# Ten of eleven feed-forward pairs by Winograd's seven products, where nine were, in a two-layer decoder trunk

## The chip, the cores and the metric

The kernel runs on one core of one Trainium2 chip. The metric is the device time of one execution in microseconds (us). The kernel before was timed three times: 2059.41, 2060.57 and 3379.97 us, median 2060.57 us. The execution that was profiled took 2059.04 us.

## The reference

The input is 512 tokens of 1024 features. Each of two layers computes, in float32,

```
x = LN(ALPHA * x + 0.5 * swiglu(x, ffn1_w13, ffn1_w2))
x = LN(ALPHA * x + mixer(x))
x = LN(ALPHA * x + 0.5 * swiglu(x, ffn2_w13, ffn2_w2))

def swiglu(x, w13, w2):
    a, b = jnp.split(x @ w13, 2, axis=-1)      # each 512 x 2816
    return (jax.nn.silu(a) * b) @ w2
```

So there are four feed-forward blocks (FFN0 and FFN1 in layer 0, FFN2 and FFN3 in layer 1). Between the two of a layer stands the mixer, a gated linear recurrence beside a gated spatial MLP; its last step is a projection of 1024 to 1024 features. The change touches the first half of each feed-forward block, `x @ w13`, and the sums that prepare the second half, `@ w2`.

## The kernel before

**Precision.** Every float32 factor is kept as a rounded part h and a rest l, and a product is three matmuls: h by h, h by l, l by h. `split` makes the parts: ScalarE copies h (L126) and VectorE subtracts it from the source to get l (L127).

**Two kinds of pairs.** The 2816 columns of a and b are 22 blocks of 128, taken as 11 pairs (k and k + 11). A **plain pair** (`proj`, L154) computes for each of its two blocks a (bank `pa`) and b (bank `pb`), each by 24 matmuls of 512 columns. A **pair by seven** (`seven_pairs`, `product`, L553) takes the two blocks, two halves of the features and two halves of the tokens as a 2 by 2 matrix product and computes it by Winograd's seven products; each is 24 matmuls of 256 columns on sums of quarters. For this VectorE adds weight quarters (`PairWeights.sum`, L533), all seven left factors are split (h_pa, l_pa, ...), and the products are combined in `evictions`. The right factors, s1 to s4, are sums of quarters of x; `x_sums` makes them once per block (tiles xr, xs, xs1h, xs1l, ...), after it has added xh and xl to get x back (L479).

**The order of a block.** Before: the pairs 8 and 9 first, as plain pairs; then a section of nine pairs by seven, whose instructions on all engines stand in the order of the program text (`pin`); then `Seven.run` (L354), which multiplies by `w2`, by seven products too. For that, the activations of each pair need sums as well (`activation_sums`, L321 to L332: 5 VectorE subtractions and two splits); three of them ran inside the section, one between the plain pairs, the other seven in `run`. Those of the plain pairs (parts th and tl) go to DRAM through GpSimd's queue and are fetched again. Sums of `w2` quarters are made in DRAM by copying and accumulating DMAs on GpSimd's queue (`sums_in_dram`, L293), one small group every `SUM_GAP` ns of the program's own clock (`Flow`).

**Around it.** Where `pin` doesn't hold, the framework's scheduler orders each engine's instructions by its own estimates. A block's x comes from the norm of the step before, transposed by TensorE per tile of 128 tokens (`to_features`, tr) and split into xh and xl; the new block's first weights (r_a, h_a, l_a and the same for b) are loaded on SP's queue. FFN0 reads x from DRAM already transposed (`first_block`). SP's queue carries all other weights; a tile class "h" of 33 slots holds the large tiles.

Of the kernel before, what the change touches and what calls it, by code (L numbers as in the profile page):

```python
# [28 lines left out]
F32 = mybir.dt.float32  # L29
# [6 lines left out]
P = 128  # L36
D = 1024
# [46 lines left out]
def trunk(ctx: ExitStack, tc, x_in, xt_in, w13, w2, w_in, w_br, w_out, ln_g, ln_b, lb_in, hgn, sgg, sgb, sgws,  # L84
# [30 lines left out]
    xh, xl = [None] * 4, [None] * 4  # L115
# [13 lines left out]
    def weights(src, name, early=False):  # L129

        raw = wk.tile([P, D], F32, tag="raw", name=f"r_{name}", bufs=NRAW)
        nc.sync.dma_start(raw, src)
# [92 lines left out]
    def out_proj(nk, lhs, w_of, c, ln, tag):  # L225

        ys = [[bank(f"y{t}{q}") for q in range(2)] for t in range(NT)]
        w = {}

        def unit(k, t, qs):  # L230
            hi, lo = w[k]
            lh, ll = lhs(k)
            ts = slice(t * P, (t + 1) * P)
            for i, (a, m) in enumerate(((lh, hi), (lh, lo), (ll, hi))):
                for q in qs:
                    PE.matmul(ys[t][q], a[:, ts], m[:, q * 512:(q + 1) * 512],  # L236
                              start=(k == 0 and i == 0), stop=(k == nk - 1 and i == 2))
# [10 lines left out]
        begin_features()  # L248
# [20 lines left out]
    class Seven:  # L269
# [3 lines left out]
        def __init__(self, w_of, order, spilled):  # L273
            self.w_of, self.order, self.spilled = w_of, order, spilled
# [30 lines left out]
        def activation_sums(self, k):  # L305
# [38 lines left out]
        def run(self, c, ln, last, due):  # L344
# [97 lines left out]
            if not last:  # L442
                begin_features()
# [25 lines left out]
    def x_sums(s):  # L469

        lo_t, hi_t = slice(0, 256), slice(256, 512)
        r = {}
        x3 = quads("xs3")
        for c in ("s2", "s1", "s3", "s4"):
            s[c] = tuple(quads(f"x{c}{v}", F32R) for v in "hl")
        for q in range(2):
            for z in (q, q + 2):
                r[z] = slot(f"xr{z}")
                V.tensor_tensor(r[z], xh[z].bitcast(F32), xl[z].bitcast(F32), op=ALU.add)  # L479
            yield 0.0, X_GAP  # L480
# [18 lines left out]
    class PairWeights:  # L499
# [14 lines left out]
        def load(self, to, col, row):  # L514
            for z, j in enumerate((self.k, self.k + NH2)):
                nc.sync.dma_start(to[:, z], self.w13_of(col + j)[:, H[row]])
# [101 lines left out]
    def ffn(l, i, last=False, first_of_all=False):  # L618
        front = [8, 9]
        by_seven = [k for k in range(NH2) if k not in front]  # L620
        order = by_seven[0:2] + front + by_seven[2:]
        seven = Seven(lambda k: w2[l, i, k], order, front)
# [26 lines left out]
        s = {}  # L649
        if first_of_all:  # L650
            glu(js[0], first_block(w13_of(js[0]), w13_of(NF + js[0])))
            s_task = flow.add(x_sums(s), 0.0)
            plain(js[1])
        else:
            first = [blocks(j, True) for j in js[:2]]
            need(0, 1)
            for z, j in enumerate(js[:2]):
# [3 lines left out]
            for z, j in enumerate(js[:2]):  # L661
                pair_of(j, first[z], 256, 256)
                glu(j, first[z])
        seven.activation_sums(front[0])
        for z, j in enumerate(js[2:]):
            args = blocks(j)
            if z == len(js) - 3:
                flow.finish(s_task)
                t = slot("rt")
                cs = [slot(f"rc{v}") for v in range(2)]  # L670
                weights_of = lambda k: PairWeights(w13_of, k, t, cs[by_seven.index(k) % 2])
                pinned[0] = True
                pw = weights_of(by_seven[0])
                pw.load_c()
                pw.load_d()
                pw.sum("t", "a", "b")
                for _ in range(AHEAD):
                    pw.split()
                pw.sum("b", "d", "b")
                pinned[0] = False  # L680
            plain(j, args)
        in_dram = flow.add(seven.sums_in_dram(order))
        pinned[0] = True
        seven_pairs(seven, s, by_seven, weights_of, pw, {0: front[1:2], 2: by_seven[0:1], 3: by_seven[1:2]})
        pinned[0] = False
        flow.finish(in_dram)
        seven.run(0.5 / ALPHA, (l, 2 * i), last, by_seven[2:])

    def gates():

        z = const.tile([P, DEPTH, NH], F32, name="lbz")
        nc.sync.dma_start(z, lb_in)
# [344 lines left out]
    def prepare():  # L1037
        tc.keep_in_program_order(nc.sync.dma_start(tril, tril_in))
        nc.sync.dma_start(ident, ident_in)
# [3 lines left out]
    def first_block(wa, wb):  # L1043

        begin_features()
# [3 lines left out]
        for _ in range(12):  # L1049
# [140 lines left out]
```

## Time and profile before

| what | value |
|---|---|
| median of the three runs | 2060.57 us |
| profiled execution | 2059.04 us, of it span 2057.2 us |
| mean granted TensorE clock | 0.998 of full speed |
| TensorE (PE) busy | 2042.1 us, 99% of the span |
| VectorE (DVE) busy | 1570.1 us, 76% |
| ScalarE (ACT) busy | 930.6 us, 45% |
| GpSimd (POOL) busy | 304.3 us, 15% |
| FFN0: first plain pair, second plain pair, nine pairs by seven | from about 6, 29.50 and 51.26 us; `run` begins at 232.69 us |

A row of the timeline names a tile by the program's name without its number: `xl<-tr,xh` is the split of a transposed bank into xl. Matmuls overlap in PE's pipeline, so the time that one adds to a chain is the distance between two starts, not the duration shown; the same holds, less strongly, on VectorE. A share of 99% says how long PE had work, not that each of its stretches was at its best rate.

### The profile page before, as it was taken

Reading aid. Unit: us, or ns where it says so; the run is one execution under the profiler, and the core shown is the slowest. Engines: PE = TensorE matmul, PEld = TensorE weight load, DVE = VectorE, ACT = ScalarE, POOL = GpSimd, SP = SyncE. Lnnn points to the kernel's source line nnn. Section 1 sums busy time; section 2 is a strip of 40 time slices with the busy share of each in tenths; the row PEclk is TensorE's granted clock in tenths of the full one; section 3 lists DMA queues with packets and bytes.
Section 4 is the critical chain, followed back from the end, with each engine's and each line's share of the span. In section 5 each row is a group of like instructions: output and inputs, shape, how many; then the busy total and the mean of one; then the engine's idle time right before and its main releaser. Section 6 shows DMA issues by size and latency. Waiting matters only on the chain. (4 is left out here: it accounts for less than half of the span.)

```text
span 2057.2 us, 32430 instructions
## 1 busy us (share of the span) xinstructions
PE 2042.1 (99%) x12640; PEld 1840.0 (89%) x12640; DVE 1570.1 (76%) x2357; ACT 930.6 (45%) x1303; POOL 304.3 (15%) x440
## 2 busy tenths in 40 slices
PE   9999999999999999999999999999999999999997
PEld 7999988888888999998899998888888889999986
DVE  7998988943435879889879989879444358898896
ACT  6444565233322544446535446642343225454563
POOL 1222002001000123210112320020010001232001
PEclk9999999999999999999999999999999999999999
DMA  8899586122242479967668986851222425899673
GB/s 264 232 254 233 170 279 231 42 82 82 83 160 96 164 212 237 260 172 252 228 187 236 248 220 192 272 201 52 82 89 86 143 93 191 212 255 239 172 256 136
DMA packets 151049, 375.11 MB, mean 182 GB/s; under 512 B 17136, under 2 KB 17392, under 8 KB 150896
## 3 DMA queue, kind: packets, MB, share of 16 engines
q1 hardware_dynamic: 102672, 242.40, 34.9%
q0 software_dynamic: 48224, 130.64, 26.4%
q8 instruction: 99, 1.62, 0.3%
q14 instruction: 54, 0.44, 0.1%
HBM read 354.10 MB, written 111.15 MB: 226 GB/s over the span
## 5 line engine op out<-in xcount | busy, mean ns | idle before, releaser
L293 POOL DMA_DIRECT2D t<-in_w_dram x176 | 145.5, 905 | 199.5 <-DMA t<-in_w_dram 107.6
L127 DVE TENSOR_TENSOR l_pc<-rc,h_pc 128x1024 fp32r<-128x1024 f32 x72 | 88.0, 1222 | 19.6 <-ACT h_pc L126 19.6
L154 PE MATMUL z<-xh,h_z 128*128 128x512 f32 x256 | 102.6, 401 | 0.0
L154 PE MATMUL z<-xh,l_z 128*128 128x512 f32 x256 | 99.8, 390 | 0.0
L154 PE MATMUL z<-xl,h_z 128*128 128x512 f32 x256 | 99.8, 390 | 0.0
L127 DVE TENSOR_TENSOR l_z<-r_z,h_z 128x1024 fp32r<-128x1024 f32 x32 | 39.2, 1225 | 72.5 <-ACT h_z L126 72.4
L126 ACT ACTIVATE h_pc<-rc 128x1024 fp32r<-128x1024 f32 x72 | 75.7, 1052 | 36.4 <-PE fB L553 34.6
L127 DVE TENSOR_TENSOR l_pa<-ra,h_pa 128x1024 fp32r<-128x1024 f32 x72 | 87.7, 1218 | 1.2 <-ACT h_pa L126 1.2
L553 PE MATMUL fA<-xh,l_pa 128*128 128x256 f32 x288 | 81.5, 283 | 0.0
L553 PE MATMUL fC<-xs1h,h_pt 128*128 128x256 f32 x288 | 81.5, 283 | 0.0
L553 PE MATMUL fC<-xs1l,h_pt 128*128 128x256 f32 x288 | 81.5, 283 | 0.0
L553 PE MATMUL fC<-xs1h,l_pt 128*128 128x256 f32 x288 | 81.5, 283 | 0.0
L553 PE MATMUL fA<-xh,h_pc 128*128 128x256 f32 x288 | 81.5, 283 | 0.0
L553 PE MATMUL fA<-xl,h_pc 128*128 128x256 f32 x288 | 81.5, 283 | 0.0
L553 PE MATMUL fA<-xh,l_pc 128*128 128x256 f32 x288 | 81.5, 283 | 0.0
L553 PE MATMUL fE<-xs3h,h_pb 128*128 128x256 f32 x288 | 81.5, 283 | 0.0
L553 PE MATMUL fE<-xs3l,h_pb 128*128 128x256 f32 x288 | 81.5, 283 | 0.0
L553 PE MATMUL fE<-xs3h,l_pb 128*128 128x256 f32 x288 | 81.5, 283 | 0.0
L553 PE MATMUL fB<-xs2h,h_pa 128*128 128x256 f32 x288 | 81.5, 283 | 0.0
L553 PE MATMUL fB<-xs2l,h_pa 128*128 128x256 f32 x288 | 81.5, 283 | 0.0
L553 PE MATMUL fB<-xs2h,l_pa 128*128 128x256 f32 x288 | 81.5, 283 | 0.0
L553 PE MATMUL fC<-xs4h,h_pd 128*128 128x256 f32 x288 | 81.5, 283 | 0.0
(360 smaller groups left out, 7370.6 us busy)
## 6 DMA issues: line engine op xcount, KB each, us to landing
t<-in_w_dram POOLq DMA_DIRECT2D x88, 512.0 KB, 9.1
t<-t POOLq DMA_DIRECT2D x88, 256.0 KB, 5.5
t<-in_w_dram POOLq DMA_DIRECT2D x88, 256.0 KB, 6.3
r_c<-in_w_dram SPq DMA_DIRECT2D x44, 512.0 KB, 5.1
r_d<-t SPq DMA_DIRECT2D x88, 256.0 KB, 4.1
rd<-in_w_dram SPq DMA_DIRECT2D x72, 256.0 KB, 6.5
ra<-in_w_dram SPq DMA_DIRECT2D x72, 256.0 KB, 5.8
rb<-in_w_dram SPq DMA_DIRECT2D x72, 256.0 KB, 6.5
```

The costliest lines, as they stand in the source:

```text
L126: pin(S.activation(hi, src, AF.Copy))
L127: pin(V.tensor_tensor(lo, src, hi.bitcast(F32), op=ALU.subtract))
L154: PE.matmul(ps[:, n0:n0 + n], a[:, cs], m[:, n0:n0 + n], start=(i == 0), stop=(i == 3 * nk - 1))
L293: tc.keep_in_program_order(nc.gpsimd.dma_start(*of(k), **kw))
L553: PE.matmul(ps[:, half[z]], a[:, ms], v, start=start, stop=(m == 3 and i == 2), skip_group_check=not (first and z == 0))
```

## The change

One pair (10) stays plain and ten are done by seven products. The plain pair's second block and the first pair's weights are put one after the other in the order of the text. `to_features` lets ScalarE copy x itself from the transposed banks into tiles xr (48 copies of 128x2x128 more), and FFN0 loads x straight into xr; the 16 additions of xh and xl go. `x_sums` makes s1 and s3 first, then s2, then s4. Six activation sums run inside the section (behind pairs 0, 1, 3, 4, 6 and 7) and five in `run`. Three pairs' parts (10, 3 and 4) go through DRAM, and those of pair 2 are kept in halves of xl and xh that the section no longer reads. `SUM_GAP` goes from 6000 to 7000, and more of SP's loads are pinned to the order of the text. In all PE issues 288 matmuls more, VectorE 32 tensor operations more, ScalarE 68 activations more, and there are 32 more DMAs.

```diff
-    SUM_GAP = 6000.0
+    SUM_GAP = 7000.0
...
-    def begin_features():
+    def begin_features(whole):
+
         for q in range(4):
             xh[q], xl[q] = slot(f"xh{q}", F32R), slot(f"xl{q}", F32R)
+        for q in range(4):
+            xr[q] = slot(f"xr{q}") if whole else None
...
             for r in range(2):
                 split(xh[2 * q + r][:, :, ts], xl[2 * q + r][:, :, ts], pv[:, r])
+            for r in range(2):
+                if xr[2 * q + r] is not None:
+                    S.activation(xr[2 * q + r][:, :, ts], pv[:, r], AF.Copy)
...
+            elif k in self.home:
+                parts = self.home.pop(k)
...
-                V.tensor_tensor(r[z], xh[z].bitcast(F32), xl[z].bitcast(F32), op=ALU.add)
...
+            V.tensor_tensor(v["s3"][q], r[:, :, lo_t], r[:, :, hi_t], op=ALU.subtract)
+            V.tensor_tensor(v["s1"][q], r[:, :, hi_t], r2[:, :, hi_t], op=ALU.subtract)
+        firsts = [xr[q][:, :, lo_t] for q in range(2)]
...
+        parts("s1")
+        yield 0.0, X_GAP
+        parts("s3")
+        for q in range(2):
+            V.tensor_tensor(v["s2"][q], firsts[q], v["s1"][q], op=ALU.subtract)
+        yield 0.0, X_GAP
+        parts("s2")
+        for q in range(2):
+            V.tensor_tensor(v["s4"][q], v["s4"][q], v["s2"][q], op=ALU.subtract)
+        yield 0.0, X_GAP
+        parts("s4")
...
-        front = [8, 9]
+        front = [10]
...
-        seven = Seven(lambda k: w2[l, i, k], order, front)
+        seven = Seven(lambda k: w2[l, i, k], order, front + by_seven[3:5])
...
         if first_of_all:
-            glu(js[0], first_block(w13_of(js[0]), w13_of(NF + js[0])))
+            pinned[0] = True
+            args = first_block(w13_of(js[0]), w13_of(NF + js[0]))
+            second = blocks(js[1])
+            pinned[0] = False
+            glu(js[0], args)
             s_task = flow.add(x_sums(s), 0.0)
-            plain(js[1])
+            flow.step(s_task)
+            flow.step(s_task)
+            pw = first_weights()
+            plain(js[1], second)
         else:
...
                 pair_of(j, first[z], 256, 256)
                 glu(j, first[z])
...
+                if z == 0:
+                    pw = first_weights()
+        flow.finish(s_task)
+        seven.home[by_seven[2]] = (xl[0][:, 0, 256:512], xl[0][:, 1, 256:512], xh[0][:, :, 256:512], xh[1][:, :, 256:512])
         in_dram = flow.add(seven.sums_in_dram(order))
         pinned[0] = True
-        seven_pairs(seven, s, by_seven, weights_of, pw, {0: front[1:2], 2: by_seven[0:1], 3: by_seven[1:2]})
+        seven_pairs(seven, s, by_seven, weights_of, pw, dict(zip((0, 1, 3, 4, 6, 7), ([v] for v in front + by_seven[0:5]))))
         pinned[0] = False
         flow.finish(in_dram)
-        seven.run(0.5 / ALPHA, (l, 2 * i), last, by_seven[2:])
+        seven.run(0.5 / ALPHA, (l, 2 * i), last, i == 1, by_seven[5:])
```

Three places show how the instructions move. The first is GpSimd's instruction list at the start of the program; its DMAs are issued in this order. `t` are the DRAM tiles of the `w2` sums, `hg` a small parameter of the mixer, th and tl the parts of a plain pair that go to DRAM. Before:

```order
L1186 UNCONDITIONAL_BRANCH
L726 DMA hg<-in_hgn_dram 128x4
L332 DMA th_327<-th_317 128x768
L332 DMA tl_328<-tl_318 128x768
L293 DMA t_75<-in_w_dram 256x512
L293 DMA t_76<-in_w_dram 256x512
L293 DMA t_83<-in_w_dram 256x512
L293 DMA t_75<-in_w_dram 256x1x512
```

With the change:

```order
L1211 UNCONDITIONAL_BRANCH
L299 DMA t_75<-in_w_dram 256x512
L299 DMA t_76<-in_w_dram 256x512
L299 DMA t_85<-in_w_dram 256x512
L299 DMA t_75<-in_w_dram 256x1x512
L299 DMA t_76<-in_w_dram 256x1x512
L299 DMA t_85<-in_w_dram 256x1x512
L752 DMA hg<-in_hgn_dram 128x4
L340 DMA th_481<-th_471 128x768
L340 DMA tl_482<-tl_472 128x768
```

The first group of `w2` copies and adds now stands at the head of the queue, where before it stood behind the parts of the first plain pair.

The second place is VectorE around the first section of FFN0, from the last result of the plain part (`r<-sa,pb`) or the first sum for the pair by seven (`rt`). `l_pa`, `l_pt`, `l_pc` and `l_pb` are the rests of the first pair's first four left factors, the xs tiles the parts of s1 to s4. Before:

```order
L639 TENSOR_TENSOR r_428<-sa,pb_344 128x2x256
L704 TENSOR_TENSOR lb<-lbmx,lbz 128x4
L533 TENSOR_TENSOR rt<-ra_447,rb_448 128x1024
L705 TENSOR_SCALAR om<-lb 128x8
L127 TENSOR_TENSOR l_pa_460<-ra_447,h_pa_459 128x1024
L127 TENSOR_TENSOR l_pt_464<-rt,h_pt_463 128x1024
L127 TENSOR_TENSOR l_pc_468<-rc_445,h_pc_467 128x1024
L533 TENSOR_TENSOR rb_448<-rd_455,rb_448 128x1024
L639 TENSOR_TENSOR r_428<-sa,pb_443 128x2x256
L533 TENSOR_TENSOR ra_447<-ra_447,rb_448 128x1024
L127 TENSOR_TENSOR l_pb_538<-rb_448,h_pb_537 128x1024
```

With the change:

```order
L548 TENSOR_TENSOR rt<-ra_262,rb_263 128x1024
L127 TENSOR_TENSOR l_pa_275<-ra_262,h_pa_274 128x1024
L127 TENSOR_TENSOR xs2l<-xr_113,xs2h 128x512
L127 TENSOR_TENSOR l_pt_279<-rt,h_pt_278 128x1024
L127 TENSOR_TENSOR l_pc_283<-rc_260,h_pc_282 128x1024
L548 TENSOR_TENSOR rb_263<-rd_270,rb_263 128x1024
L127 TENSOR_TENSOR xs2l<-xr_114,xs2h 128x512
L505 TENSOR_TENSOR xr_113<-xr_113 128x2x256
L505 TENSOR_TENSOR xr_114<-xr_114 128x2x256
L654 TENSOR_TENSOR r_238<-sa,pb_235 128x2x256
L127 TENSOR_TENSOR xs4l<-xr_113,xs4h 128x512
L127 TENSOR_TENSOR xs4l<-xr_114,xs4h 128x512
```

The first pair's weight sums and rests now stand between the sums and rests of x, before the last result of the plain part; `ra` and `l_pb` follow behind the rows shown.

The third place is VectorE at the end of layer 0's mixer. `x,sums<-y` adds the mixer's output to x for a tile of tokens, `xl<-tr,xh` splits the transposed x, and l_a, l_b are the rests of the first plain block of FFN1. Before:

```order
L196 SCALAR_TENSOR_TENSOR x_6195,sums<-y_6064,x_6195 128x512
L127 TENSOR_TENSOR l_a_6462<-r_a_6459,h_a_6461 128x1024
L202 TENSOR_SCALAR nm<-sums 128x1
L127 TENSOR_TENSOR l_b_6468<-r_b_6465,h_b_6467 128x1024
L127 TENSOR_TENSOR l_a_6476<-r_a_6473,h_a_6475 128x1024
L208 SCALAR_TENSOR_TENSOR x_6195<-x_6195,nm,lng 128x512 x2
L209 SCALAR_TENSOR_TENSOR x_6195<-x_6195,rstd,lnb 128x512 x2
L127 TENSOR_TENSOR xl_6200<-tr_6379,xh_6199 128x2x128
L127 TENSOR_TENSOR xl_6204<-tr_6391,xh_6203 128x2x128
L196 SCALAR_TENSOR_TENSOR x_6197,sums<-y_6065,x_6197 128x512
```

With the change:

```order
L208 TENSOR_SCALAR nm<-sums 128x1
L214 SCALAR_TENSOR_TENSOR x_6292<-x_6292,nm,lng 128x512 x2
L215 SCALAR_TENSOR_TENSOR x_6292<-x_6292,rstd,lnb 128x512 x2
L127 TENSOR_TENSOR xl_6297<-tr_6484,xh_6296 128x2x128
L127 TENSOR_TENSOR xl_6301<-tr_6498,xh_6300 128x2x128
L202 SCALAR_TENSOR_TENSOR x_6294,sums<-y_6162,x_6294 128x512
L127 TENSOR_TENSOR xl_6299<-tr_6484,xh_6298 128x2x128
L127 TENSOR_TENSOR xl_6303<-tr_6498,xh_6302 128x2x128
L202 SCALAR_TENSOR_TENSOR x_6294,sums<-y_6163,x_6294 128x512
L127 TENSOR_TENSOR l_a_6571<-r_a_6568,h_a_6570 128x1024
L208 TENSOR_SCALAR nm<-sums 128x1
L127 TENSOR_TENSOR l_b_6577<-r_b_6574,h_b_6576 128x1024
```

The rests of the first block's weights now stand behind the last addition of the mixer's output (y_6163); before they stood ahead of the norm of the tile of tokens before it.

## Rows read from the trace of the kernel before

**Rows 1.** The page: span, then busy time of each engine.
```profile
span 2057.2 us, 32430 instructions
PE 2042.1 (99%) x12640; PEld 1840.0 (89%) x12640; DVE 1570.1 (76%) x2357; ACT 930.6 (45%) x1303; POOL 304.3 (15%) x440
```

**Rows 2.** Waits of PE: who for whom, total us, times, longest us.
```profile
PE pE L354 <- DVE l_d L127: 1.6, 4, 0.7
PE pA L354 <- DVE l_c L127: 0.6, 2, 0.3
```

**Rows 3.** Chain of waits in FFN3: start us, us, what; 24 matmuls each.
```profile
1748.81 5.44 PE pa L154 x24
1762.57 2.88 PE fC L553 x24
```

**Rows 4.** PE's timeline: start us, us, line, tile; firsts of stretches.
```profile
29.50 0.39 PE L154 MATMUL pa<-xh,h_a 128*128 128x512 f32 x1
51.26 0.28 PE L553 MATMUL fA<-xh,h_pa 128*128 128x256 f32 x1
232.69 0.40 PE L354 MATMUL pA<-h_b,th 128*128 128x512 f32 x1
715.16 0.40 PE L154 MATMUL pa<-xh,h_a 128*128 128x512 f32 x1
1052.12 0.40 PE L154 MATMUL pa<-xl,h_a 128*128 128x512 f32 x1
```

**Rows 5.** Windows, two pairs: length; PE, PEld, DVE, ACT, POOL busy; clock, DMA.
```profile
100.00:120.00 20.00, 20.00 (x169) 20.00 (x168) 19.28 (x25) 10.11 (x13) 4.14 (x6) 1.00 0.95 228
180.00:200.00 20.00, 20.00 (x169) 20.00 (x168) 17.25 (x19) 9.40 (x11) 4.98 (x6) 1.00 0.91 237
```

**Rows 6.** VectorE's timeline, FFN1: start us, us, line, tiles, shapes.
```profile
712.08 0.68 DVE L127 TENSOR_TENSOR xs4l<-xr,xs4h 128x512 fp32r<-128x512 f32 x1
712.68 0.42 DVE L127 TENSOR_TENSOR tl<-r,th 128x256 fp32r<-128x256 f32 x1
713.02 2.35 DVE L479 TENSOR_TENSOR xr<-xh,xl 128x1024 f32<-128x1024 f32 x2
715.29 0.68 DVE L483 TENSOR_TENSOR xs<-xr 128x512 f32<-128x512 f32 x1
```

**Rows 7.** GpSimd's timeline at the start; in brackets idle time and releaser.
```profile
1.24 0.74 POOL L726 DMA_DIRECT2D hg<-in_hgn_dram  x1 [0.81 <-POOLq L1175]
35.20 0.56 POOL L332 DMA_DIRECT2D th<-th  x1 [33.22 <-ACT th L126]
37.46 1.69 POOL L293 DMA_DIRECT2D t<-in_w_dram  x3
```

**Rows 8.** Windows at the start (columns as in Rows 5).
```profile
7.50:10.00 2.50, 2.06 (x7) 1.11 (x8) 1.40 (x3) 1.90 (x3) 0.00 (x0) 1.00 1.05 387
10.00:12.50 2.50, 2.50 (x13) 2.03 (x11) 2.49 (x5) 2.35 (x4) 0.00 (x0) 1.00 1.07 411
```

**Rows 9.** ScalarE's and PE's timelines in the first block.
```profile
11.38 2.66 ACT L126 ACTIVATE xh<-xt 128x512 fp32r<-128x512 f32 x4
...
15.90 0.39 PE L1080 MATMUL pa<-xh,h_a 128*128 128x512 f32 x1
```

**Rows 10.** The page's DMA issues: count, KB each, us to landing.
```profile
t<-in_w_dram POOLq DMA_DIRECT2D x88, 512.0 KB, 9.1
```

**Rows 11.** VectorE's timeline, where the work for FFN0's section would begin.
```profile
18.95 0.69 DVE L639 TENSOR_TENSOR r<-sa,pb 128x512 f32<-128x512 f32 x1 [0.69 <-ACT sa L638]
```

**Rows 12.** VectorE's and PE's timelines at the end of layer 0's mixer.
```profile
683.51 1.23 DVE L127 TENSOR_TENSOR l_a<-r_a,h_a 128x1024 fp32r<-128x1024 f32 x1
691.63 0.68 DVE L196 SCALAR_TENSOR_TENSOR x<-y,x 128x512 f32<-128x512 f32 x1
...
689.90 0.39 PE L236 MATMUL y<-h_wo,yt 128*128 128x512 f32 x1
690.13 0.28 PE L154 MATMUL pa<-xh,h_a 128*128 128x256 f32 x1
```

**Rows 13.** VectorE's timeline: last splits of x in FFN1 and FFN2.
```profile
704.28 0.74 DVE L127 TENSOR_TENSOR xl<-tr,xh 128x256 fp32r<-128x256 f32 x2
1042.61 0.42 DVE L127 TENSOR_TENSOR xl<-tr,xh 128x256 fp32r<-128x256 f32 x1
```

**Rows 14.** Groups by line, all of the span: count, busy us, mean ns.
```profile
L126 ACT ACTIVATE xh<-tr 128x256 fp32r<-128x256 f32 x80 | 28.6, 382 | 44.8 <-DVE xl L127 25.3 <-PE tr L172 18.8
```

More of the change, by code (lines that the diff above doesn't have):

```diff
@@ L131, in weights @@
         raw = wk.tile([P, D], F32, tag="raw", name=f"r_{name}", bufs=NRAW)
-        nc.sync.dma_start(raw, src)
+        pin(nc.sync.dma_start(raw, src))
         if early:
@@ L247, in out_proj @@
         xs = load_rows()
-        begin_features()
+        begin_features(True)
         for t in range(NT):
@@ L273, in __init__ @@
         def __init__(self, w_of, order, spilled):
-            self.w_of, self.order, self.spilled = w_of, order, spilled
+            self.w_of, self.order, self.spilled, self.home = w_of, order, spilled, {}
             self.r, self.t, self.last = {}, {}, None
@@ L342, in fetched, with run @@
             return hl[0][:, 0], hl[1][:, 0], hl[0][:, 1:3], hl[1][:, 1:3]
-        def run(self, c, ln, last, due):
+        def run(self, c, ln, last, whole, due):
             ops = {}
@@ L442, in run @@
             if not last:
-                begin_features()
+                begin_features(whole)
             sums = [small("sums", 2) for _ in range(NT)]
@@ L515, in load @@
             for z, j in enumerate((self.k, self.k + NH2)):
-                nc.sync.dma_start(to[:, z], self.w13_of(col + j)[:, H[row]])
+                pin(nc.sync.dma_start(to[:, z], self.w13_of(col + j)[:, H[row]]))
         def load_d(self):
@@ L649, in ffn, with weights_of, first_weights @@
         s = {}
-        if first_of_all:
-            glu(js[0], first_block(w13_of(js[0]), w13_of(NF + js[0])))
+        bufs = []
+        def weights_of(k):
+            return PairWeights(w13_of, k, bufs[0], bufs[1 + by_seven.index(k) % 2])
+        def first_weights():
+            pinned[0] = True
+            bufs.extend(slot(f"r{v}") for v in ("t", "c0", "c1"))
+            pw = weights_of(by_seven[0])
+            pw.load_c()
+            pw.load_d()
+            pw.sum("t", "a", "b")
+            for _ in range(AHEAD):
+                pw.split()
+            pw.sum("b", "d", "b")
+            pinned[0] = False
+            return pw
+        if first_of_all:
+            pinned[0] = True
+            args = first_block(w13_of(js[0]), w13_of(NF + js[0]))
+            second = blocks(js[1])
+            pinned[0] = False
+            glu(js[0], args)
             s_task = flow.add(x_sums(s), 0.0)
-            plain(js[1])
+            flow.step(s_task)
+            flow.step(s_task)
+            pw = first_weights()
+            plain(js[1], second)
         else:
-            first = [blocks(j, True) for j in js[:2]]
+            first = [blocks(j, True) for j in js]
             need(0, 1)
-            for z, j in enumerate(js[:2]):
+            for z, j in enumerate(js):
                 pair_of(j, first[z], 0, 256)
@@ L660, in ffn @@
             s_task = flow.add(x_sums(s), 2000.0)
-            for z, j in enumerate(js[:2]):
+            for z, j in enumerate(js):
                 pair_of(j, first[z], 256, 256)
                 glu(j, first[z])
[L664 to L681, printed above, removed]
+                if z == 0:
+                    pw = first_weights()
+        flow.finish(s_task)
+        seven.home[by_seven[2]] = (xl[0][:, 0, 256:512], xl[0][:, 1, 256:512], xh[0][:, :, 256:512], xh[1][:, :, 256:512])
         in_dram = flow.add(seven.sums_in_dram(order))
         pinned[0] = True
-        seven_pairs(seven, s, by_seven, weights_of, pw, {0: front[1:2], 2: by_seven[0:1], 3: by_seven[1:2]})
+        seven_pairs(seven, s, by_seven, weights_of, pw, dict(zip((0, 1, 3, 4, 6, 7), ([v] for v in front + by_seven[0:5]))))
         pinned[0] = False
         flow.finish(in_dram)
-        seven.run(0.5 / ALPHA, (l, 2 * i), last, by_seven[2:])
+        seven.run(0.5 / ALPHA, (l, 2 * i), last, i == 1, by_seven[5:])
     def gates():
         z = const.tile([P, DEPTH, NH], F32, name="lbz")
-        nc.sync.dma_start(z, lb_in)
+        tc.keep_in_program_order(nc.sync.dma_start(z, lb_in))
         mx = const.tile([P, NH], F32, name="lbmx")
@@ L1038, in prepare @@
         tc.keep_in_program_order(nc.sync.dma_start(tril, tril_in))
-        nc.sync.dma_start(ident, ident_in)
+        tc.keep_in_program_order(nc.sync.dma_start(ident, ident_in))
         gates()
@@ L1043, in first_block @@
     def first_block(wa, wb):
-        begin_features()
+        begin_features(True)
         zero = wk.tile([P, T], F32, tag="sa", name="zero", bufs=NSA)
@@ L1052, in first_block @@
         w = [[wk.tile([P, D], F32R, tag="w", name=f"{c}_{v}0", bufs=NW) for c in "hl"] for v in "ab"]
-        rx = [wk.tile([P, D], F32, tag=tag, name=f"xt{q}", bufs=n)
-              for q, (tag, n) in enumerate((("raw", NRAW), ("raw", NRAW), ("rs", 2), ("rs", 2)))]
+        rx = [v.rearrange("p a t -> p (a t)") for v in xr]
         def weight(v, z):
-            nc.sync.dma_start(rw[v][:, H[z]], (wa, wb)[v][:, H[z]])
+            pin(nc.sync.dma_start(rw[v][:, H[z]], (wa, wb)[v][:, H[z]]))
             split(w[v][0][:, H[z]], w[v][1][:, H[z]], rw[v][:, H[z]])
         def feature(q, z):
-            nc.sync.dma_start(rx[q][:, H[z]], xt_in[q, :, H[z]])
+            pin(nc.sync.dma_start(rx[q][:, H[z]], xt_in[q, :, H[z]]))
             split(xh[q][:, z, :], xl[q][:, z, :], rx[q][:, H[z]])
```

30 lines of the change are left out of this document (11 added, 19 removed).

## The prediction

> **What bounds the kernel now.** I read the page first, then the waits of PE, the chain of waits, PE's timeline and the busy time by windows. PE is busy 2042.1 of 2057.2 us [rows 1], and the windows inside the section of pairs by seven show it busy 20.00 of 20.00 us at a granted clock of 1.00 [rows 5]. The longest waits of PE for VectorE are 1.6 us and 0.6 us in all [rows 2]. So the kernel is bound by the number of matmuls and their spacing. What saves PE time shows in the end almost in full; what other engines do shows only where they are late for PE, and VectorE is close to that: it is busy 19.28 of 20.00 us where a pair has activation sums and 17.25 where it has none [rows 5].
>
> **The gain.** A plain pair costs from 29.50 to 51.26, 21.76 us [rows 4]; by the chain, 4 groups of 24 matmuls of 5.44 us [rows 3], the same. Nine pairs by seven take from 51.26 to 232.69 us [rows 4], 20.16 us each: 7 products of 24 matmuls of 2.88 us, 120 ns a matmul of 256 columns against 227 ns for 512 [rows 3]. One pair that changes sides gains 21.76 − 20.16 = 1.60 us in each of four blocks, **6.4 us**. The Trainium skill ("TensorE: Matmul & The Clock Gate", section "Back-to-back issue gap") gives 262 cycles for 256 columns and 518 for 512, which would be 18.3 and 20.7 us for the pairs and 9.5 us over four blocks by an estimate from that page; the rows here disagree, with 120 and 227 ns, and the sum uses them.
>
> **What it costs, place by place.** VectorE's prices are distances between starts: 1.14 us for 128x1024 (713.02 to 715.29 is two), 0.60 for 128x512, 0.34 for 128x256 [rows 6].
>
> *The start.* GpSimd's queue issues `hg` at 1.24 us, then waits until 35.20 for th, and the first `w2` copies go out at 37.46 [rows 7]. With the change three copies of 512 KB and three adds stand first and wait for nothing, so they go out at about 1 us, while SP's queue loads twelve pieces of 256 KB, 3.1 MB. The DMA engines are full then: share 1.05 to 1.07, 387 to 411 GB/s [rows 8]. So 1.5 MB of copies take bandwidth from the first block, about 3.8 us at 400 GB/s if they take all of their share before it ends. The cover: ScalarE's last four splits of x end by 14.04, and PE gets to that part at 15.90 [rows 9], 1.9 us later. A copy takes 9.1 us to land [rows 10], so not all of it falls on SP's loads. Between −1 (nothing moved, the section's later adds eased) and +5 I take **+1.0**: half of 3.8 less half the cover.
>
> *The start of FFN0's section.* It now begins near 29.3 us rather than 51.26 [rows 4], and VectorE has to make x's sums and the first left factors by then. From 18.95 [rows 11], in the order of the instructions: r 0.60, l_b 1.14, six tensor operations for s3, s1 and s2 and four rests 0.60 each, rt 1.14, l_pa 1.14: about 29.0. Then xs2l, l_pt, l_pc, rb, xs2l, two for s4, r, two rests of s4, ra, l_pb: five of 1.14 and seven of 0.60, 38.9. Product 3 needs l_pb at 29.3 + 3 × 2.88 = 37.9 plus two matmuls, 38.2: **0.7** late. By the second pair's first product six more of 1.14, the sums of pair 10 (2.3 us in all), the small operations of the gates and l_pa add up to some 51.4 against a need of 49.5 + 0.7: another 1.1. Of this 1.8 I take **+1.5** (bounds 0 and +3: with perfect packing, and with as much again in waits for ScalarE).
>
> *The end of the mixer, twice.* Before, l_a of the next block is made at 683.51, 6.6 us ahead of its first matmul at 690.13 [rows 12]. Now it stands behind the addition of the last y (before: 691.63 to 692.2 [rows 12]) and takes 1.14 more, to 693.3 or, with y finished at 690.1 and two things less ahead, 692.1 at best. PE has the transposes of a token tile and the first matmuls of pb in between, about 1.1 us from 690.1, and pb waits for h_b, which is behind ScalarE's new copies of x (0.38 us each, the price of an xh copy [rows 14]). Of the wait of 2.0 to 3.2 us, PE covers 1.1. Bounds 0 and +2.1, taken **+1.0** each, **+2.0** for FFN1 and FFN3.
>
> *The sections of FFN1 to FFN3.* The last xl comes at 704.28 in FFN1, the point from which the change would start the section is 715.16 (the second plain pair before); 10.9 us. In FFN2 it is 1042.61 and 1052.12, 9.5 us [rows 4, 13]. The 16 additions of xh and xl (1.14 each) are gone, 4.6 us a block, and the weight sums and first rests, some 8 us, come in. FFN1 and FFN3 cost 0, covered by these 10.9 us; FFN2 **+0.5** (0 to +1.2).
>
> *Inside the sections.* Six pairs of ten rather than three of nine carry activation sums. VectorE then needs 19.28/20 of a pair, 19.4 of 20.16 us [rows 5], so PE still covers it: 0, if VectorE never waits more than 0.7 us in such a pair. ScalarE's 48 more copies (18 us) and POOL's more spills lie beside 10.11 of 20 busy [rows 5]: 0. `run` loses two activation sums (4.6 us of VectorE each block); its waits for l_d and l_c, 2.2 us in all [rows 2], may shrink, −2.2 at most, 0 taken. The 3 tiles through DRAM rather than two are fetched inside the section, far ahead of `run`: 0. A longer SUM_GAP gives 24 groups of 7 us, 168 us from 29, over before the section ends at 231: 0.
>
> **The sum.** −6.4 + 1.0 + 1.5 + 2.0 + 0.5 = **−1.4 us** on the profiled 2059.04, 2057.6. The median of the runs is 1.5 above the profiled run (one of three runs far off), so on that base it is 2059.2; I say **2058.5**. With all bounds at their low end −9.6, 2049; at the high end +7, 2066.
>
> **The rivals.**
> *All of the gain (0.15).* Each place is covered: SP's loads win at the start, the scheduler's order is slack that PE doesn't need. For it: PE waits are tiny everywhere now [rows 2]; against: three places move work from ahead of PE to just in time. −6.4 gives 2052.6 to 2054.2.
> *POOL's copies starve the start (0.15).* DMA is full there already [rows 8] and the first block has only 1.9 us of slack. If the copies get an equal share of the engines for as long as they run, SP's 3.1 MB at about 200 GB/s instead of 400 come some 3.8 us later by the copies and as much by the adds behind them, less the cover: +4 to +6 beside the 4.0 of the other places, 2063 to 2066. It decides if the last xt lands more than 1.9 us later than now. The Trainium skill ("DMA: Bandwidth & Descriptors", section "Queues, rings and completion order") says that a DMA engine serves the queue rows with work in turn, packet by packet, which would make the share equal; no row here shows two queues in full demand at once.
> *VectorE becomes the bound in the section (0.12), slower than before.* A pair with sums leaves 0.7 us. If VectorE waits 1.2 us in each (for ScalarE's h part, behind an activation of Silu, or for a bank), it ends each of six pairs 0.5 late: 24 × 0.5 = 12 us, 2059 − 1.4 + 12 = 2070. In FFN0 it starts the section already behind. For: pairs 0 and 1, 3 and 4, 6 and 7 are neighbours, and only a pair without sums (2.8 us of slack by 17.25 of 20 [rows 5]) lets it recover. Against: before, pairs 2 and 3 were neighbours with sums, and no wait of PE at L553 is among the long ones [rows 2].
> *The change doesn't do what it says (0.03).* A tile not free in time (33 slots hold four more x tiles) would hold SP's weights and cost a fixed stall per block: 2060 to 2070.
> The rest, **0.55**, is my forecast, 2055 to 2062.
>
> **Range and chances.** The range 2052.5 to 2067 takes in the first three cases but the far side of VectorE as bound, and leaves out some 0.2. A change of less than 2%, 41 us, counts as none here: the whole gain is 6.4, with the waits in `run` 8.6, so faster by 2% can't come from any case (0.01, for what I haven't seen), and slower needs stalls ten times those summed, say a fallen granted clock for long (0.02). Same: 0.97.
>
> **What would show it.** The waits of PE would show a wait of about 1 us for l_pb or l_pa in FFN0's section, one of 1 us each for l_a or h_b at the start of FFN1 and FFN3, and in the first 15 us a wait for xt or h_a; PE's timeline would show FFN0's section starting at 29 to 31 us and `run` some 201.6 us later if no sums are late. A window in a pair with sums with PE under 19.9 of 20 would show VectorE as the bound. The forecast is wrong if PE waits sum to under 2 us or over 9 us more than before, or if a pair by seven in the section takes over 20.3 us.

## The result: slower by 0.4%, and where the time went

The kernel with the change took 2067.28 us (median of six runs, 2065.99 to 2069.68), the kernel before 2059.59 us; the ratio is 1.0039 (95% interval 1.0025 to 1.0053). The forecast was 2058.5 with a range to 2067.0: it lies outside, by a little, and on the other side of no change. The profiled execution is the longest of the six, 2069.68 us; its span is 10.4 us longer than that of before, while the medians differ by 7.7, so the table below holds some 3 us that a typical execution lacks. These are the page's first rows and the waits of PE (who waited for whom: us in total, times, longest) of the changed kernel, beside [rows 1] and [rows 2]. In its line numbers L1105 is the first block's product, L568 a product of a pair by seven, L362 `run`.

```profile
span 2067.6 us, 33160 instructions
PE 2042.2 (99%) x12928; PEld 1855.2 (90%) x12928; DVE 1595.6 (77%) x2389; ACT 958.3 (46%) x1371; POOL 312.3 (15%) x448
```

```profile
PE pa L1105 <- ACT xh L126: 6.7, 3, 4.0
PE pb L154 <- ACT h_b L126: 3.4, 2, 1.7
PE fA L568 <- ACT h_pa L126: 2.7, 2, 2.1
PE fA L568 <- ACT r L581: 0.9, 1, 0.9
```

Before, the largest waits inside the stretches came to 1.6 and 0.6 us in all (the wait of 1.1 us ahead of the first instruction is the same in both); now three places have more. The two waits for l_d and l_c in `run` are gone from the list. PE's timeline gives the borders of the stretches (start us, us, line, tiles), to be set against [rows 4]:

```profile
40.70 0.28 PE L568 MATMUL fA<-xh,h_pa 128*128 128x256 f32 x1
248.04 0.40 PE L362 MATMUL pA<-h_b,th 128*128 128x512 f32 x1
730.62 0.28 PE L568 MATMUL fA<-xh,h_pa 128*128 128x256 f32 x1
1064.18 0.28 PE L568 MATMUL fA<-xh,h_pa 128*128 128x256 f32 x1
```

From such firsts of all stretches, with the second plain pair of before counted to its section so that both columns hold ten pairs:

| stretch, us | before | after | difference | forecast |
|---|---|---|---|---|
| start to the end of FFN0's first plain pair | 29.50 | 40.70 | +11.2 | +1.0 |
| FFN0, ten pairs | 203.2 | 207.3 | +4.1 | −0.1 |
| FFN1, first plain pair | 25.0 | 26.7 | +1.7 | +1.0 |
| FFN3, first plain pair | 25.2 | 28.3 | +3.1 | +1.0 |
| FFN2, first plain pair | 25.3 | 25.1 | −0.2 | 0 |
| FFN1, FFN2, FFN3, ten pairs each | 609.2 | 607.1 | −2.1 | −4.3 |
| four times `run`, the last with the end | 441.3 | 433.9 | −7.4 | 0 |
| both mixers | 698.5 | 698.5 | 0.0 | 0 |

The sum is +10.4. The gain of a pair is there: FFN1's ten pairs took 201.9 us, 20.19 each. What ate it is mostly the first 30 us. Two rows are larger here than in other traces with the same code in that place: FFN0's section begins at 39.75 us in e3_add and 39.44 in e4_run7, and FFN3's first plain pair takes 26.8 us in e1_hold, e4_run7, e5_hold_dma and e6_gates_late.

**The start.** GpSimd's timeline of the changed kernel, to be read against [rows 7]; then windows of 5 us (columns as in [rows 5]) against [rows 8]:

```profile
1.22 1.91 POOL L299 DMA_DIRECT2D t<-in_w_dram  x3 [0.80 <-POOLq L1200]
9.68 1.12 POOL L299 DMA_DIRECT2D t<-in_w_dram  x1 [6.54 <-DMA t<-in_w_dram]
11.59 1.04 POOL L299 DMA_DIRECT2D t<-in_w_dram  x1 [0.79 <-DMA t<-in_w_dram]
13.62 1.02 POOL L299 DMA_DIRECT2D t<-in_w_dram  x1 [0.99 <-DMA t<-in_w_dram]
```

```profile
5.00:10.00 5.00, 1.31 (x8) 0.71 (x6) 0.51 (x1) 0.37 (x1) 0.32 (x1) 1.00 0.95 341
10.00:15.00 5.00, 4.46 (x11) 2.70 (x11) 2.17 (x4) 2.26 (x5) 3.22 (x4) 0.66 1.06 368
15.00:20.00 5.00, 3.03 (x13) 2.13 (x12) 2.20 (x4) 1.74 (x3) 0.26 (x1) 1.00 1.09 274
20.00:25.00 5.00, 4.08 (x10) 2.52 (x10) 1.76 (x3) 1.26 (x2) 0.00 (x0) 0.63 1.09 279
25.00:30.00 5.00, 5.00 (x17) 3.99 (x16) 1.92 (x2) 3.19 (x4) 0.00 (x0) 0.69 1.04 349
```

By their share the DMA engines are as full as before, but not with SP's loads. The DMA view of the first 20 us (queue: packets, MB, share of the engines' time, q1 that of SP's loads and q0 GpSimd's; then an issue's count, KB each, median us to landing), first after, then before:

```profile
q1 hardware_dynamic: 1771, 3.42, 47.7%
q0 software_dynamic: 834, 2.36, 43.1%
xr<-in_xt_dram SPq DMA_DIRECT2D x8, 256.0 KB, 12.3
```

```profile
q1 hardware_dynamic: 2898, 5.98, 83.4%
xt<-in_xt_dram SPq DMA_DIRECT2D x8, 256.0 KB, 6.2
```

GpSimd's queue took 43.1% of the engines' time and SP's 47.7%, where SP had 83.4% before; a piece of x took 12.3 us to land instead of 6.2. ScalarE's last split of x, which ended at 14.04 before [rows 9], now ended at 25.97:

```profile
25.34 0.63 ACT L126 ACTIVATE xh<-xr 128x512 fp32r<-128x512 f32 x1 [1.54 <-DMA xr<-in_xt_dram]
```

The same view of two windows of the changed kernel, 5 to 10 us (the copies) and 15 to 20 us (the adds), shows that the adds cost more than the copies:

```profile
q0 software_dynamic: 287, 1.06, 57.3%
q1 hardware_dynamic: 354, 0.65, 37.2%
```

```profile
q0 software_dynamic: 315, 0.61, 66.0%
q1 hardware_dynamic: 311, 0.76, 43.3%
```

Per megabyte GpSimd's queue took 54% of the engines' time of such a window as copies and 108% as adds, and from 15 to 20 us all that the engines moved was 274 GB/s at a share of 1.09, as against 411 at 1.07 in [rows 8]. PE ran dry: it was busy 1.31 of 5.00 us from 5 to 10, waited 7.2 us for xh and xl in all, and behind each of the two long waits its granted clock is 0.66 and 0.63 in the mean of a window, a mixture of stretches at 2.4 and at 1.2 GHz (matmuls 0.23 us apart, and 0.43). By busy time and clock of the windows the lower clock cost, as an estimate, 0.34 × 4.46 + 0.37 × 4.08 + 0.31 × 5.00 = 4.6 us. With the waits, less the 0.5 that the first block had before, this makes 11.3, near the 11.2 of the table; as the first matmul began 0.6 us earlier than before, some 0.5 us are not assigned.

### The profile page after: what moved, and what is told of

The parts are those of the page before. It is cut to its first block, busy times and chain, and to the rows that moved or that the text cites. A ratio compares the mean times of both kernels' runs of the same rounds, so it can differ in the third digit from the quotient of the medians.

```text
span 2067.6 us, 33160 instructions
## 1 busy us (share of the span) xinstructions
PE 2042.2 (99%) x12928; PEld 1855.2 (90%) x12928; DVE 1595.6 (77%) x2389; ACT 958.3 (46%) x1371; POOL 312.3 (15%) x448
## 4 chain that ended last, share of the span: by engine, by line
PE 90%; DVE 5%; issue 1%; DMA 1%; ACT 1%; POOL 1%; SPq 0%; POOLq 0%; DVEq 0%; ACTq 0%
PE fE L568 11%; PE fC L568 10%; PE fA L568 10%; PE z L154 8%; PE pA L362 6%; PE pC L362 6%; PE fB L568 5%; PE y L154 4%; PE pB L362 3%; PE pF L362 3%; PE pE L362 3%; PE y L242 2%; PE q L154 2%; PE f L154 2%; PE i L774 2%; PE g L154 2%
## 5 line engine op out<-in xcount | busy, mean ns | idle before, releaser
L127 DVE TENSOR_TENSOR l_pc<-rc,h_pc 128x1024 fp32r<-128x1024 f32 x80 | 97.6, 1221 | 18.4 <-ACT h_pc L126 18.3
L127 DVE TENSOR_TENSOR l_pa<-ra,h_pa 128x1024 fp32r<-128x1024 f32 x80 | 97.4, 1217 | 0.0
L568 PE MATMUL fA<-xh,h_pa 128*128 128x256 f32 x320 | 90.8, 284 | 2.7 <-ACT h_pa L126 2.7
L568 PE MATMUL fE<-xh,h_pc 128*128 128x256 f32 x320 | 91.7, 287 | 0.7 <-DVE b L588 0.6
L568 PE MATMUL fA<-xh,h_pc 128*128 128x256 f32 x320 | 90.8, 284 | 1.1 <-ACT r L581 0.9
L568 PE MATMUL fE<-xl,h_pc 128*128 128x256 f32 x320 | 91.2, 285 | 0.0
L568 PE MATMUL fE<-xh,l_pc 128*128 128x256 f32 x320 | 91.1, 285 | 0.0
L568 PE MATMUL fA<-xh,l_pa 128*128 128x256 f32 x320 | 90.7, 283 | 0.0
L568 PE MATMUL fB<-xs2h,h_pa 128*128 128x256 f32 x320 | 90.6, 283 | 0.0
L568 PE MATMUL fC<-xs1h,h_pt 128*128 128x256 f32 x320 | 90.6, 283 | 0.0
L568 PE MATMUL fC<-xs1l,h_pt 128*128 128x256 f32 x320 | 90.6, 283 | 0.0
L568 PE MATMUL fC<-xs1h,l_pt 128*128 128x256 f32 x320 | 90.6, 283 | 0.0
L568 PE MATMUL fB<-xs2l,h_pa 128*128 128x256 f32 x320 | 90.6, 283 | 0.0
L568 PE MATMUL fB<-xs2h,l_pa 128*128 128x256 f32 x320 | 90.6, 283 | 0.0
L568 PE MATMUL fC<-xs4h,h_pd 128*128 128x256 f32 x320 | 90.6, 283 | 0.0
L568 PE MATMUL fC<-xs4l,h_pd 128*128 128x256 f32 x320 | 90.6, 283 | 0.0
```

The lines of the kernel that those rows point to most:

```text
L127: pin(V.tensor_tensor(lo, src, hi.bitcast(F32), op=ALU.subtract))
L568: PE.matmul(ps[:, half[z]], a[:, ms], v, start=start, stop=(m == 3 and i == 2), skip_group_check=not (first and z == 0))
```

## The experiments

The first four take the change apart. The copies at the start were held back, without other changes of order:

```diff
+        if first_of_all:
+            tc.keep_in_program_order(G.tensor_copy(small("hold"), seven.room(front[0])[:, 1, 0:1]))
         in_dram = flow.add(seven.sums_in_dram(order))
```

> The change, with one GpSimd copy of one column that reads the result of the second plain block, placed ahead of the first group of w2 copies in FFN0; so those copies go out behind the first loads. Theory S (the copies at the head of GpSimd's queue take bandwidth from the first loads, PE waits for them and its clock falls): FFN0's section starts at 29.5 to 30.5 us instead of 40.70 and the time falls by 10 to 11 us, to 2056 to 2057. Rival P (the pinned order of SP's loads, or the loading of x into xr, is what is late): the section starts at 39 to 41 us, 2066 to 2068. For the 4.5 us of stalls at 47 to 66 us inside that section: if VectorE's chain makes them (V) they stay at 3 to 6 us behind the earlier start; if the late loads make them (L), they vanish and the time is 2052.

Measured: 2057.24 us (median of 11 runs), FFN0's section starts at 29.20. Theory S holds and rival P falls: 11.5 us of the start are these six DMAs. The stalls near 50 us stayed (V; 3.3 us): late loads are not their cause. But the runs lie in two groups, six at 2055.6 to 2057.2 and five at 2062.4 to 2064.9. The one profile is of the longer kind; GpSimd's and ScalarE's timelines in it show a wait of about the difference:

```profile
35.20 10.60 POOL L709 COPY hold<-r 128x1 f32<-128x1 f32 x1 [33.22 <-DVE r L654]
200.98 0.56 POOL L340 DMA_DIRECT2D th<-th  x1
205.95 0.60 ACT L581 ACTIVATE r<-fA 128x512 f32<-128x512 f32 x1 [8.70 <-DMA th<-th]
```

The copy of one column, the first such instruction of GpSimd in the program, took 10.6 us. At 201 us a pair's parts go to DRAM behind the `w2` sums; ScalarE's eviction needs the tile that they leave and waits 8.7 us, and PE 5.4. That a late queue is the reason is a theory here; e5_hold_dma below tests it.

The other side of the same test puts the six DMAs at the head of GpSimd's queue in the kernel before:

```diff
+        in_dram = flow.add(seven.sums_in_dram(order))
+        in_dram[0] = 1e12
         if first_of_all:
+            flow.step(in_dram)
+            flow.step(in_dram)
+            in_dram[0] = 1e12
...
-        in_dram = flow.add(seven.sums_in_dram(order))
+        in_dram[0] = flow.clock
```

> The kernel before with nothing changed but the first group of w2 copies and adds of FFN0 (six DMAs of 512 KB) issued at the head of GpSimd's queue, as the change does. Theory S: the first plain block ends 10 to 12 us later and the time is 2059.6 + 11 = 2069 to 2072. Rival P: these copies are not the cause, 2059 to 2061.

Measured: 2073.21 us, 13.5 more than before (ratio 1.0065, 1.0052 to 1.0077), 11.2 of it ahead of 62.42 us, where its section starts (51.26 before). Another 2.5 us lie in the four `run`s, 0.5 to 0.8 each; why is not shown. The windows show the same picture, the clock with it:

```profile
5.00:10.00 5.00, 1.68 (x11) 1.17 (x9) 0.73 (x2) 0.42 (x2) 0.18 (x1) 1.00 0.95 312
10.00:15.00 5.00, 3.49 (x8) 2.26 (x9) 1.75 (x3) 2.03 (x4) 2.97 (x4) 0.70 1.06 378
```

So these six DMAs alone are enough to delay the start, whatever else the change does.

The third undoes ScalarE's copies of x:

```diff
-            for r in range(2):
-                if xr[2 * q + r] is not None:
-                    S.activation(xr[2 * q + r][:, :, ts], pv[:, r], AF.Copy)
...
+        if add[0]:
+            for z in (0, 2, 1, 3):
+                V.tensor_tensor(xr[z], xh[z].bitcast(F32), xl[z].bitcast(F32), op=ALU.add)
...
+        add[0] = True
```

> The change without ScalarE's 48 copies of x: VectorE adds xh and xl again in FFN1 to FFN3, at the head of the sums of x. Theory C (ScalarE's copies delay h_b at the start of FFN1 and FFN3): the waits of 1.8 us for h_b in both, and the fall of the clock behind the one in FFN3, go: -5 us; the adds cost 4.6 us of VectorE per block, of which 1 us a block shows: about 2065. Rival O (the scheduler's order on VectorE and PE, l_a and h_b behind the last addition of y, is the cause): the waits stay at 1 to 2 us each and the adds come on top, 2068 to 2073.

Measured: 2075.55 us, 8.3 more than the change. The waits for h_b went, as C says (the plain pairs of FFN1 and FFN3 take 25.1 us again), worth 4.8 us against the changed kernel's trace and 3.3 against the traces in which FFN3's pair takes 26.8. But the adds cost 4.0 to 4.2 us per block, not 1: the ten pairs of FFN1 took 205.9 us instead of 201.9. The total forecast of both theories was wrong on this price; of the 4.6 us of VectorE that the adds take at the start of a section, nearly all shows. ScalarE's copies are worth about 12 us and cost 3.3 to 4.8. As the order of the instructions around them changed too, this run doesn't part theory C from rival O; e7_copies_late does.

The fourth moves two activation sums back:

```diff
-        seven = Seven(lambda k: w2[l, i, k], order, front + by_seven[3:5])
+        seven = Seven(lambda k: w2[l, i, k], order, front)
...
-        seven_pairs(seven, s, by_seven, weights_of, pw, dict(zip((0, 1, 3, 4, 6, 7), ([v] for v in front + by_seven[0:5]))))
+        seven_pairs(seven, s, by_seven, weights_of, pw, dict(zip((0, 1, 3, 4), ([v] for v in front + by_seven[0:3]))))
...
-        seven.run(0.5 / ALPHA, (l, 2 * i), last, i == 1, by_seven[5:])
+        seven.run(0.5 / ALPHA, (l, 2 * i), last, i == 1, by_seven[3:])
```

> The change with the activation sums of pairs 3 and 4 moved back from the section into run (four in the section, seven in run, one pair through DRAM). Theory R (run became 1.6 to 2.1 us shorter in every block because VectorE has two sums less there): each run is 1.3 to 2 us longer again, 2072 to 2075. Rival (run gained through the wider SUM_GAP or other loads): run stays at 106.6 us and the time at 2066 to 2068.

Measured: 2075.82 us. The four `run`s are 1.9 to 2.5 us longer each, 8.9 in all, as theory R says. Of the two waits of PE that the change had removed, the one for l_d is back, and two others stand beside it:

```profile
PE pA L362 <- DVE l_b L127: 3.0, 4, 0.8
PE pA L362 <- ACT h_b L126: 1.1, 2, 0.7
PE pE L362 <- DVE l_d L127: 0.7, 2, 0.5
```

So the sums whose waits came to 2.2 us in [rows 2] were worth 7.4 us to the change: PE's timeline shows further gaps of 0.1 to 0.2 us between matmuls that the list of waits leaves out.

All that follow start from a cleaner hold: a small DMA that reads the first plain block's result, at 19 us.

```diff
+            held = dram.tile([P, 16], F32, name="held", tag="held", bufs=1)
+            tc.keep_in_program_order(nc.gpsimd.dma_start(held, seven.room(front[0])[:, 0, 0:16]))
```

> The change, with the first group of w2 copies held behind a small DMA that reads the result of the first plain block (at about 19 us), in place of the GpSimd copy of e1_hold, which itself took 10.6 us (35.20 to 45.75) and left GpSimd's queue late. Theory Q (the wait of 5.4 us for a spilled tile near 206 us in part of e1_hold's runs came from a queue that was late): no run has it, the time is 2055 to 2057 in all runs and FFN0's section starts at 29 to 30 us. Rival (the spill is late whenever the section starts early): some runs are 6 us longer again, 2062 to 2065.

Measured: 2055.64 us (ratio to before 0.998, 0.9971 to 0.9989); all runs but one far off lie at 2054.5 to 2057.1, in one group, as theory Q says. The `w2` copies now go out at 19.50 us and not at 45.75; how much of the late queue was the copy's own 10.6 us, and how much the later block that it waited for, these runs don't part. The next edit is for the largest stall of FFN0's section:

```diff
-    prep = flow.add(prepare(), 30000.0)
+    prep = flow.add(prepare(), 135000.0)
```

> e5_hold_dma with the gates' small operations (an Exp with its table load on ScalarE, ten small ones on VectorE) moved from the first two pairs of FFN0's section to about 135 us of the program's clock. Theory G (they stand ahead of h_pa of pair 1 on ScalarE and VectorE): the stall of 2.2 us at 49 us shrinks by 1.3 to 2.3 us, 2053 to 2054.5. Rival V (the sums of x and of pair 10 alone make VectorE late): it shrinks by under 0.7 us, 2055 to 2056.5.

Measured: 2061.18 us, 5.5 more than e5_hold_dma. Its timelines show a gain and a larger loss. The stall of 2.24 us at 48.75 (the distance between two starts, less the usual 0.12) became 0.72 at 46.98, as G says. In the changed kernel ScalarE and PE stood like this there:

```profile
58.41 0.63 ACT L126 ACTIVATE th<-s 128x512 fp32r<-128x512 f32 x1 [4.46 <-DVE s L330]
59.06 1.28 ACT L723 ACT_TABLE_LOAD   x1
60.35 0.21 ACT L723 ACTIVATE lbz<-lbz 128x8 f32<-128x8 f32 x1
60.47 1.04 ACT L126 ACTIVATE h_pa<-ra 128x1024 fp32r<-128x1024 f32 x1
61.56 0.39 PE L568 MATMUL fA<-xh,h_pa 128*128 128x256 f32 x1 [2.07 <-ACT h_pa L126]
```

h_pa, which PE waits for, is behind the sums of pair 10 (th, which waits 4.46 us for VectorE) and behind the table and the Exp of the gates. But the edit had moved the load of their input too, behind SP's other loads, and VectorE waited for it:

```profile
139.22 0.16 DVE L722 TENSOR_TENSOR lbmx<-lbz 128x4 f32<-128x4 f32 x1 [11.82 <-DMA lbz<-in_lb_dram]
```

The 4 KB were issued at 126.08 and landed some 13 us later; until then all that follows on VectorE stood still. PE waited 6.8 us for it, and its granted clock was 0.50 from 139 to 145 us.

At the end of the mixer, the copies of x were put behind the splits of the whole token tile in the text:

```diff
+        pvs = []
...
+            pvs.append(pv)
+            yield 4 * 109.0, 0.0
+        for q, pv in enumerate(pvs):
             for r in range(2):
                 if xr[2 * q + r] is not None:
                     S.activation(xr[2 * q + r][:, :, ts], pv[:, r], AF.Copy)
-            yield 4 * 109.0, 0.0
```

> e5_hold_dma with ScalarE's copies of x to xr put behind the splits of the whole token tile in the text, which lets the scheduler put l_a and h_b of the next block ahead again, in the order of the kernel before. Theory C (copies and order at the end of the mixer make PE wait for h_b, 1.8 us in FFN1 and FFN3, and lower its clock in FFN3): 3.5 to 5 us less than e5_hold_dma, 2051 to 2052.5. Rival (the wait moves to l_a or to xl): less than 1.5 us gained.

Measured: 2051.72 us, 3.9 less than e5_hold_dma and 0.9962 of before (0.9949 to 0.9976). In the changed kernel the rows on ScalarE, VectorE and PE after the last y were

```profile
704.66 1.21 ACT L181 ACTIVATE xr<-tr 128x256 f32<-128x256 f32 x4 [0.56 <-DVE xl L127]
705.73 1.08 ACT L126 ACTIVATE h_b<-r_b 128x1024 fp32r<-128x1024 f32 x1
705.48 1.22 DVE L127 TENSOR_TENSOR l_a<-r_a,h_a 128x1024 fp32r<-128x1024 f32 x1
706.86 0.38 PE L154 MATMUL pb<-xh,h_b 128*128 128x256 f32 x1 [1.72 <-ACT h_b L126]
```

and with the edit, ahead of its first block at 690.23, as in [rows 12],

```profile
683.65 1.06 ACT L126 ACTIVATE h_a<-r_a 128x1024 fp32r<-128x1024 f32 x1
685.73 1.06 ACT L126 ACTIVATE h_b<-r_b 128x1024 fp32r<-128x1024 f32 x1
684.75 1.23 DVE L127 TENSOR_TENSOR l_a<-r_a,h_a 128x1024 fp32r<-128x1024 f32 x1 [0.81 <-ACT h_a L126]
```

with no wait of PE left there; the plain pairs of FFN1 and FFN3 take 24.8 us instead of 26.8. The copies were not too many; they stood in the wrong place, and the scheduler's order followed them.

The next run has the edits of e6_gates_late and e7_copies_late together.

> Both together. If the places are independent, the two gains add: 2049 to 2051, faster than the kernel before by 9 to 11 us (0.4 to 0.5%).

Measured: 2057.49 us, 5.8 more than e7_copies_late: the late load of the gates' input costs the same here (PE waits 7.2 us for l_pt), so the gains did not add. The next edit leaves the load where it was and puts a delay of the program's own clock only before the computing:

```diff
-        gates()
+        z = const.tile([P, DEPTH, NH], F32, name="lbz")
+        tc.keep_in_program_order(nc.sync.dma_start(z, lb_in))
+        yield 0.0, 105000.0
+        gates(z)
```

> e7_copies_late with the gates' input loaded early, as in the change, and only their computing moved to about 135 us. In e6_gates_late the stall at 49 us fell from 2.2 to 0.7 us, but VectorE then waited 11.8 us for that input, whose load had moved too. Theory (that load alone made the 7 us wait): no wait at 141 us, and 1.0 to 2.0 us less than e7_copies_late, 2049.7 to 2050.7. Rival (the Exp with its table load costs as much in any place of the section): 2051 to 2053.

Measured: 2049.18 us, 2.5 less than e7_copies_late and somewhat more than forecast; no wait near 141 us. But the edit didn't move the computing to 135 us: the trace has the first of the gates' operations at 45.77 us, the Exp at 49.24 and the last of them near 70. What it did is to let h_pa of pair 1 go ahead of the table load (in e7_copies_late the load is at 46.24 and h_pa at 47.65):

```profile
46.89 1.04 ACT L126 ACTIVATE h_pa<-ra 128x1024 fp32r<-128x1024 f32 x1
47.95 1.28 ACT L726 ACT_TABLE_LOAD   x1
```

The stall there fell to 0.70 us, and FFN0's section from 205.6 to 203.9. So the order on ScalarE is what the gain shows; the rival, on the price of the Exp further on, wasn't put to the test. Last, the activation sums of FFN0 and FFN2 one pair later:

```diff
-        seven_pairs(seven, s, by_seven, weights_of, pw, dict(zip((0, 1, 3, 4, 6, 7), ([v] for v in front + by_seven[0:5]))))
+        seven_pairs(seven, s, by_seven, weights_of, pw, dict(zip((0, 1, 3, 4, 6, 7) if i else (1, 2, 4, 5, 7, 8), ([v] for v in front + by_seven[0:5]))))
```

> e9_gates_split with the six activation sums of FFN0 and FFN2 behind pairs 1, 2, 4, 5, 7 and 8 instead of 0, 1, 3, 4, 6 and 7. Theory V (VectorE is behind at the start of these two sections, and the sums of pair 10 behind pair 0 keep it there): the stalls left near 47 us in FFN0 and at 14 to 16 us into FFN2's section, about 1.1 and 1.2 us, go: 2047.5 to 2049. Rival (the spill of pair 4 behind pair 8 is then late for its tile's next use): a wait of some us near the end of the section, 2050 to 2056.

Measured: **2046.14 us** (2045.78 to 2046.44), 0.9931 of before (0.9917 to 0.9945) and faster than every other version here. The stalls of pair 1 in FFN0 and FFN2 are gone (their sections take 202.3 and 202.0 us), no spill is late, and this is all that the list of PE's waits for other engines still holds beside the first instruction:

```profile
PE fA L571 <- ACT r L584: 0.4, 1, 0.4
PE pE L365 <- DVE l_d L127: 0.3, 1, 0.3
```

## Why the prediction was wrong, step by step

**The start is the step that failed.** It was put at +1.0, between −1 and +5, and measured +11.2 (taken away by e1_hold, put into the kernel before by e2_before_early). The mechanism stood among the rivals, with 0.15 and +4 to +6, and its own sign came: the last piece of x was split 11.9 us later than before, not 1.9. Three things made the step's price too small. Only the three copies, 1.5 MB, were counted in the step, though the instruction order showed three adds of the same size right behind; in the first 20 us GpSimd's queue moved 2.36 MB, and a byte added took about twice the engines' time of a byte copied, which the rival, too, didn't have. The landing time of 9.1 us [rows 10] was read as cover, though a transfer that lands slowly in a full system makes its neighbour slow as well: SP's pieces of x went from 6.2 to 12.3 us. And the price had no term for the clock, though PE that waits 4 us in a row came out of it at 0.66: 4.6 us for the lower clock in all; the rival lacked this term as well. As the share of DMA was above 1.0 already [rows 8], that rival should have been the forecast. The Trainium skill ("DMA: Bandwidth & Descriptors", section "Queues, rings and completion order") says that a DMA engine takes the queues with work in turn. The trace agrees: from 15 to 20 us, with work on both, it has 315 packets of GpSimd's queue and 311 of SP's.

**FFN0's section** was put at +1.5 and cost 5.7: 4.1 + 1.6 of the pair's gain. One of the two places was right (pair 1's first product waited 2.1 us; product 3 hardly waited for l_pb), but the sum held VectorE alone. What was late was ScalarE: its h_pa stood behind th, which waits for VectorE, and behind the gates' table load, 1.28 us (e6_gates_late, e9_gates_split, e10_sums_later); in pair 0 the eviction r came 0.9 us late. The clock took a part here as well: behind the wait for h_pa matmuls ran 0.21 us apart instead of 0.12 from 62.9 to 65.6 us, some 1.4 us more. **FFN2's section**, put at +0.5 and at most +1.2, cost 1.9, 0.3 + 1.6: of this, e10_sums_later takes away 1.3 by putting the sums of pair 10 one pair later.

**The ends of the mixers**, +1.0 each, measured +1.7 and +3.1; the working (l_a and h_b behind the last y) was right, and the size was low: PE waited 1.7 us for h_b in each. In FFN3 the wait was followed by a granted clock of 0.69 for 5 us, some 1.5 us more, in this trace and in none of the four others with the same wait (e1_hold, e4_run7, e5_hold_dma, e6_gates_late):

```profile
1726.00:1731.00 5.00, 4.67 (x27) 4.67 (x28) 4.52 (x7) 3.85 (x7) 1.71 (x2) 0.69 0.57 175
```

**The gain of 6.4** was right: FFN1's and FFN3's sections took 201.9 us for their ten pairs, where 201.6 were expected, as against 203.2 for one plain and nine. **VectorE as the bound** of the section didn't come: with six sums FFN1's section has 0.3 us of gaps. **`run`**, put at 0 and −2.2 at most, gave −7.4 (e4_run7), because gaps that the list of waits leaves out went too. By this luck the total missed the range by only 0.3 us: the other steps were under by 19 us together. The prediction's own sign of being wrong came: PE's listed waits sum to 15.9 us as against 3.8, 12.1 more, where over 9 more was to show it. That the change is worth less than 2% either way was right.

## What to carry to other kernels

An instruction without a dependency isn't free: a queue that was held back by a wait may have protected the loads of another queue, and when the wait goes, the price is both the lost bandwidth and the lower clock of an engine that runs dry. When work is moved, look for what now stands behind it on every engine's queue, the small loads and table loads too. And where the prediction finds a full resource, let the sharing of it be the forecast, not a rival.

## What the hardware showed unexpectedly

- A stall of PE can cost more than its length, and the same stall need not. Behind waits of 4.0 and 2.0 us at the start the granted clock fell to 0.66 and 0.63 in windows of 5 us, and behind 1.7 us at FFN3 to 0.69; behind the same wait at FFN3 it stayed at 1.00 in e1_hold, e4_run7, e5_hold_dma and e6_gates_late. Two runs have a wait of 2.08 us for h_pa near 48.75 us; these are their windows behind it, e5_hold_dma first, then e7_copies_late:

```profile
50.00:53.00 3.00, 3.00 (x16) 3.00 (x16) 2.97 (x4) 2.82 (x3) 0.00 (x0) 0.51 0.86 268
50.00:53.00 3.00, 3.00 (x28) 3.00 (x27) 2.97 (x4) 2.82 (x3) 0.00 (x0) 1.00 0.80 235
```

  So the length of the wait alone doesn't decide it. What does stays open.
- GpSimd's first copy of 128x1 took 10.6 us; the issue of a DMA on its queue that served the same end took 0.56 us (e5_hold_dma). The cause wasn't looked for.
- A load of 4 KB on SP's queue, the gates' input, landed 3.9 to 5.6 us after its issue in the five executions in which GpSimd's queue moved nothing meanwhile (before, the change, e1_hold, e3_add, e4_run7), though SP's own loads held 61 to 91% of the DMA engines' time. It took 8.1 us where GpSimd's queue held 23% (e2_before_early) and 12.8 to 13.9 us in the six others, where that queue held 71 to 82%. This fits the sharing of the start, but no run was made to test it.
